# Expert weights as a dense matrix: two 128-column products per token accumulated in PSUM

## Chip, cores and metric

One NeuronCore of one Trainium2 chip runs the whole program. The metric is device time in microseconds (us) of one execution. For the kernel before, three runs are shown, with a median of 1796.3 us (1794.24 to 1799.25). A profiled execution of its own was recorded beside them.

## The reference, cut to what matters

A transformer block and a second block run over 256 tokens. The change lies in the last layer of the second block, `peer`, in which every token picks 8 x 16 = 128 of 16384 one-neuron experts through two tables of 128 keys, and sums their outputs:

```
experts = e1 * N_KEYS + e2                      # N_KEYS = 128
g = softmax(cs)                                 # 128 weights a token
act = gelu(einsum('td,tkd->tk', xt, u_tab[et])) * gt
out = einsum('tk,tkd->td', act, v_tab[et])
```

## The kernel before, in words

The kernel doesn't gather. It computes the activation of **all** 16384 experts for all 256 tokens, multiplies it by a dense matrix of weights that is zero where an expert wasn't picked, and multiplies the result by all of `v_tab`. Everything is 32-bit; a matrix product is made of three (`mm3`, lines 303 to 306): each operand is split into a rounded high half and the low rest, both of type fp32r, and high x high, high x low and low x high are added up in PSUM.

Three stages matter here.

- **Experts in.** `experts_in` (line 1389) takes two tiles of `u_tab` (128 experts each), makes two products of 8 x 3 = 24 matmuls of 256 columns with the tokens (`gemm_w`, lines 308 to 312; in the trace lines 304, 305 and 306), applies gelu on ScalarE (line 1396) and stores the pair to DRAM. Each tile of 128x1024 weights comes through `Stream`: a load on the SP queue, a rounding copy on ScalarE (line 250, tile `wh`) and a subtraction on VectorE (line 252, tile `wl`), four tiles ahead, each with four buffers. There are 64 such pairs; the first ones run beside the routing, the rest beside the dense weights.
- **Dense weights.** `weights_dense` (line 1508) is a generator that is stepped from inside the loop of line 1572: after each `gemm_w`, `paced` (line 1547) steps it about three times, so its instructions stand in every engine's queue between those of two expert tiles. It takes one token a step. For four tokens VectorE makes four one-hot matrices of the first index (line 1518, tile `oh1`, two buffers). For each token VectorE makes a 128x256 tile (line 1523, tile `ow`, six buffers): the one-hot of the second index times the high half of the weight, and beside it the same times the low half. Four steps later (`LAG`, line 29) TensorE multiplies the two (line 1533): one matmul of 256 columns, 128 of the high and 128 of the low half, with the first one-hot as the stationary operand. Two tokens fill a PSUM bank of 512 columns (tag `acc`, three banks). When a bank is full ScalarE copies the low parts to `gd` (line 1538), and VectorE adds the high parts to them (line 1539).
- **Experts out.** When all tokens are done, `act_split` (line 1560) multiplies the stored activations by `gd` on GpSimd (line 1564), splits them, and the products with `v_tab` follow.

The order on each engine is the order in which the program issues (`manual_schedule`): an instruction that waits holds up all that stands behind it on its engine.

Of the kernel before, what the change touches and what calls it, by code (L numbers as in the profile page):

```python
# [16 lines left out]
ALU = mybir.AluOpType  # L17
# [4 lines left out]
T = 256  # L22
# [7 lines left out]
ONE = 4  # L30
# [253 lines left out]
def body(ctx, tc, a, o, upto=99):  # L284
    nc = tc.nc
# [6 lines left out]
    def psum(tag):  # L292
        return PS.tile([128, 512], F32, tag=tag, name=tag, bufs={"mm": 2, "acc": 3, "od": 1, "tr": 2}[tag])

    def accs():
        return [psum("acc"), psum("acc"), psum("acc"), psum("od")]
# [37 lines left out]
    def gemm_rows(acc, w, xh, xl, start, stop):  # L334
        h, lo = w
        for tt in range(2):
            ts_ = slice(tt * 128, tt * 128 + 128)
            for hf in range(2):
                cs = slice(hf * 512, hf * 512 + 512)
                mm3(acc[2 * tt + hf], xh[:, ts_], xl[:, ts_], h[:, cs], lo[:, cs], start, stop)  # L340

    def split(h, lo, src, eng=None):
        nc.scalar.copy(h, src)  # L343
        (eng or nc.vector).tensor_tensor(lo, src, h.bitcast(F32), op=ALU.subtract)  # L344
# [32 lines left out]
    def gain(i, pool):  # L377
        g = pool.tile([128, D], F32, tag="gain", name="gain", bufs=1)
        nc.gpsimd.dma_start(g, a["gains"][i:i + 1, :].to_broadcast([128, D]))
        return g  # L380
# [283 lines left out]
    with tc.tile_pool(name="mix", bufs=1) as MP:  # L664
# [251 lines left out]
        for n, (s, g) in enumerate(MIX_ORDER):  # L916
# [6 lines left out]
            if n == 2:  # L923
                pump.add(subln())
                for gg in range(3):
                    pt = psum("mm")
# [19 lines left out]
        for c in range(8):  # L946
            pt = psum("mm")
# [11 lines left out]
        for b in range(4):  # L959
            if b % 2 == 0:  # L960
                w = ws.next()
            pt = psum("tr" if b % 2 else "mm")
# [11 lines left out]
        g = gain(POSTM, MP)  # L974
# [88 lines left out]
    with tc.tile_pool(name="b2", bufs=1) as BP:  # L1063
# [277 lines left out]
        for i in range(4):  # L1341
            pt = psum("mm")
# [4 lines left out]
            t = th[:, 2 * i:2 * i + 2, :]  # L1347
# [10 lines left out]
        for c in range(8):  # L1358
            pt = psum("mm")
# [29 lines left out]
    def experts_in(i, between=pump.step):  # L1389
        pt = psum("mm")  # L1390
        gemm_w(pt[:, :T], ws.next(), xs_x)
        between()
        gemm_w(pt[:, T:], ws.next(), xs_x)
        st = PP.tile([128, 2, T], F32, tag="st", name="st", bufs=2)
        last[i] = st
        nc.scalar.activation(st, pt.rearrange("p (e t) -> p e t", e=2), AF.Gelu_apprx_tanh)  # L1396
        if i < 62:
            nc.scalar.dma_start(stored[i // 4][:, 2 * (i % 4):2 * (i % 4) + 2, :], st)
# [3 lines left out]
    with tc.tile_pool(name="route", bufs=1) as RP:  # L1402
# [3 lines left out]
        v = RP.tile([128, 2, 16, 16], F32, name="v")  # L1406
# [22 lines left out]
        for b in range(16):  # L1429
            if b < 2:  # L1430
                pt = first[b]
            else:
                pt = psum("mm")
# [69 lines left out]
    with tc.tile_pool(name="dense", bufs=1) as GP:  # L1503
        gd = GP.tile([128, 128, T], F32, name="gd")

        wp = GP.tile([128, 2, 128], F32R, name="wp")

        def weights_dense():

            o1s, ohs = {}, {}  # L1510
            for t in range(T + LAG):
                if t < T:
                    tt, tl = divmod(t, 128)
                    if tl == 0:
                        split(wp[:, 0], wp[:, 1], eT[tt][:, 2])
                    if t % ONE == 0:
                        o1 = GP.tile([128, ONE, 128], F32R, tag="oh1", name="oh1", bufs=2)
                        nc.vector.tensor_tensor(o1, iota[:, None, :].to_broadcast([128, ONE, 128]),  # L1518
                                                eT[tt][:, 0, tl:tl + ONE, None].to_broadcast([128, ONE, 128]),
                                                op=ALU.is_equal)  # L1520
                        o1s[t // ONE] = o1
                    oh = GP.tile([128, 2, 128], F32R, tag="ow", name="oh2", bufs=6)
                    nc.vector.scalar_tensor_tensor(oh, iota[:, None, :].to_broadcast([128, 2, 128]),  # L1523
                                                   eT[tt][:, 1, tl:tl + 1],
                                                   wp[:, :, tl:tl + 1].bitcast(F32).to_broadcast([128, 2, 128]),
                                                   op0=ALU.is_equal, op1=ALU.mult)
                    ohs[t] = oh
                u = t - LAG
                if u >= 0:
                    if u % 2 == 0:  # L1530
                        pt = psum("acc")
                    oh = ohs.pop(u)
                    nc.tensor.matmul(pt[:, u % 2 * T:u % 2 * T + T], o1s[u // ONE][:, u % ONE],  # L1533
                                     oh.rearrange("p n e -> p (n e)"), start=True, stop=True)
                    if u % 2 == 1:
                        v = pt.rearrange("p (t n e) -> p n e t", t=2, n=2)
                        g = gd[:, :, u - 1:u + 1]
                        nc.scalar.copy(g, v[:, 1])  # L1538
                        nc.vector.tensor_tensor(g, v[:, 0], g, op=ALU.add)  # L1539
                yield  # L1540

        pump.add(weights_dense())
        left = 128 - 2 * n_in[0]
        total = T + LAG
        busy = left - 4

        def paced(i):
            for _ in range(min(i + 1, busy) * total // busy - min(i, busy) * total // busy):
                pump.step()

        sv = {}

        def fetch(b):
            if b < 16:
                sv[b] = P0.tile([128, 8, T], F32, tag="lT" if b % 2 else "hT", name="sv")
                nc.gpsimd.dma_start(sv[b][:, :8 if b < 15 else 4, :], stored[b])

        order = list(range(124, 128)) + list(range(124))

        def act_split(n):  # L1560
            e = order[n]
            src = last[e // 2] if e >= 124 else sv[e // 8][:, e % 8 - e % 2:e % 8 - e % 2 + 2, :]
            if e % 2 == 0:
                nc.gpsimd.tensor_tensor(src, src, gd[:, e:e + 2, :], op=ALU.mult)  # L1564
            ah = GP.tile([128, T], F32R, tag="ow", name="ah", bufs=6)
            al = GP.tile([128, T], F32R, tag="ow", name="al", bufs=6)
            split(ah, al, src[:, e % 2])
            if e % 8 == 7 and e < 120:
                fetch(e // 8 + 2)
            return ah, al  # L1570

        for i in range(left // 2):
            experts_in(n_in[0] + i, lambda: paced(2 * i))
            paced(2 * i + 1)
            if i == left // 2 - 2:
                pump.drain()
                ws.pool_every = 0
                nxt = [act_split(0), act_split(1)]
        fetch(0)
        fetch(1)  # L1580
        acc = accs()
        for n in range(126):
            nxt.append(act_split(n + 2))
            ah, al = nxt.pop(0)
            gemm_rows(acc, ws.next(), ah, al, n == 0, False)
        gf = P0.tile([128, D], F32, tag="raw", name="gf", bufs=RAW)
        nc.scalar.dma_start(gf, a["gains"][FINAL:FINAL + 1, :].to_broadcast([128, D]))
        x2 = [P0.tile([128, D], F32, tag="raw", name="x2", bufs=RAW) for tt in range(2)]
        for tt in range(2):
            nc.scalar.dma_start(x2[tt], res[tt * 128:(tt + 1) * 128, :])  # L1590
        finish(acc, [(ws.next(), *nxt[n]) for n in range(2)])
        jk = P0.tile([128, 1024], F32, tag="wh", name="jk", bufs=NH)
        ys = [P0.tile([128, D], F32, tag="wl", name="ys", bufs=NL) for tt in range(2)]
        rs = [None, None]

        def scaled(tt, hf):
            y = ys[tt][:, HALVES[hf]]
            if hf:
                nc.scalar.activation(y, y, AF.Copy, scale=rs[tt])
            else:  # L1600
                nc.vector.tensor_scalar(y, y, rs[tt], None, op0=ALU.mult)
            (nc.scalar if tt and hf else nc.sync).dma_start(o[tt * 128:tt * 128 + 128, HALVES[hf]], y)

        for tt in range(2):
            fn = RowNorm(GP, lambda hf: x2[tt][:, HALVES[hf]], jk[:, :512])
            for hf, sl in enumerate(HALVES):
                nc.vector.tensor_tensor(x2[tt][:, sl], acc[2 * tt + hf], x2[tt][:, sl], op=ALU.add)
                fn.half(hf)
            if tt:
                scaled(0, 0)  # L1610
                scaled(0, 1)
            for sl in HALVES:
                nc.vector.tensor_tensor(ys[tt][:, sl], x2[tt][:, sl], gf[:, sl], op=ALU.mult)
            rs[tt] = fn.root()
        for hf in range(2):
            scaled(1, hf)
# [19 lines left out]
```

## Time and profile before

| what | us |
|---|---|
| median of 3 runs | 1796.3 |
| profiled execution, its own time | 1792.96 |
| span of the profiled execution, first to last instruction | 1791.1 |
| PE busy (97% of the span) | 1729.7 |
| DVE busy (74%) | 1332.6 |
| ACT busy (52%) | 936.1 |
| POOL busy (18%) | 319.1 |

PE is TensorE's matmuls, PEld its weight loads, DVE VectorE, ACT ScalarE, POOL GpSimd. The dense weights are made from 1146 to 1424 us of the span. The granted clock of TensorE is 0.991 over the span, 1.0 being 2.4 GHz. A duration of an instruction reaches from its start to its end; neighbours on one engine overlap, so the time that an instruction takes up in a full queue is the distance from its start to the next one's, which is shorter. A timeline merges neighbours of one line: "0.97 ... x8" is the time from the first start to the last end of eight.

### The profile page before, as it was taken

Reading aid. Unit: us, or ns where it says so; the run is one execution under the profiler, and the core shown is the slowest. Engines: PE = TensorE matmul, PEld = TensorE weight load, DVE = VectorE, ACT = ScalarE, POOL = GpSimd, SP = SyncE. Lnnn points to the kernel's source line nnn. Section 1 sums busy time; section 2 is a strip of 40 time slices with the busy share of each in tenths; the row PEclk is TensorE's granted clock in tenths of the full one; section 3 lists DMA queues with packets and bytes.
Section 4 is the critical chain, followed back from the end, with each engine's and each line's share of the span. In section 5 each row is a group of like instructions: output and inputs, shape, how many; then the busy total and the mean of one; then the engine's idle time right before and its main releaser. Section 6 shows DMA issues by size and latency. Waiting matters only on the chain.

```text
span 1791.1 us, 30504 instructions
## 1 busy us (share of the span) xinstructions
PE 1729.7 (97%) x11790; PEld 1581.5 (88%) x11794; DVE 1332.6 (74%) x2177; ACT 936.1 (52%) x1515; POOL 319.1 (18%) x249
## 2 busy tenths in 40 slices
PE   8999999999999999999899889899999999999998
PEld 7999888999899987997799889899999988888886
DVE  5665668855665645888767999899999977776766
ACT  5544556545464435685545345455555545545554
POOL 3000133221300101000003344100000033333332
PEclk9999999999999999999999999999999999999999
DMA  7656453444476653553255456566665677777775
GB/s 235 191 174 196 148 164 106 138 134 156 162 216 190 198 166 117 167 188 106 91 180 191 140 189 219 199 195 190 200 198 191 199 249 252 243 241 240 244 239 173
DMA packets 93410, 332.08 MB, mean 185 GB/s; under 512 B 10552, under 2 KB 10707, under 8 KB 90960
## 3 DMA queue, kind: packets, MB, share of 16 engines
q1 hardware_dynamic: 79488, 287.73, 50.0%
q0 software_dynamic: 3696, 21.67, 3.6%
q10 hardware_dynamic: 10080, 20.71, 3.2%
q8 instruction: 93, 1.52, 0.4%
q14 instruction: 53, 0.43, 0.1%
HBM read 311.73 MB, written 18.35 MB: 184 GB/s over the span
## 4 chain that ended last, share of the span: by engine, by line
PE 62%; DVE 26%; issue 4%; ACT 4%; DMA 3%; POOL 1%; ACTq 0%; POOLq 0%; SPq 0%; DVEq 0%
PE mm L304 10%; PE mm L306 9%; PE mm L305 9%; PE acc L306 7%; PE acc L305 7%; PE acc L304 7%; DVE wl L252 7%; DVE oh L1523 5%; DVE gd L1539 2%; PE od L304 2%; PE od L305 2%; PE od L306 2%; DVE oh L1518 2%; ACT wh L250 2%; DMA raw<-in_us_dram 1%
## 5 line engine op out<-in xcount | busy, mean ns | idle before, releaser
L252 DVE TENSOR_TENSOR wl<-raw,wh 128x1024 fp32r<-128x1024 f32 x502 | 651.9, 1302 | 281.7 <-ACT wh L250 279.6
L306 PE MATMUL mm<-hT,wl 128*128 128x256 f32 (+1 forms) x2496 | 706.5, 283 | 10.7 <-DVE wl L252 10.7
L304 PE MATMUL mm<-hT,wh 128*128 128x256 f32 (+1 forms) x2496 | 715.0, 286 | 1.7 <-ACT rxp L1227 1.3
L250 ACT CAST wh<-raw 128x1024 fp32r<-128x1024 f32 x544 | 570.4, 1052 | 262.1 <-DMA raw<-in_us_dram 73.2
L305 PE MATMUL mm<-lT,wh 128*128 128x256 f32 (+1 forms) x2496 | 706.3, 283 | 0.0
L306 PEld LDWEIGHTS mm<-hT,wl 128*128 128x128 f32 x2496 | 475.5, 191 | 11.7 <-DVE wl L252 11.7
L304 PEld LDWEIGHTS mm<-hT,wh 128*128 128x128 f32 x2496 | 475.1, 190 | 10.4 <-issue 5.5
L305 PEld LDWEIGHTS mm<-lT,wh 128*128 128x128 f32 x2496 | 473.9, 190 | 3.4 <-issue 1.4
L306 PE MATMUL acc<-wh,al 128*128 128x512 f32 x516 | 202.1, 392 | 0.5 <-DVE al L344 0.5
L304 PE MATMUL acc<-wh,ah 128*128 128x512 f32 x516 | 202.0, 391 | 0.0
L305 PE MATMUL acc<-wl,ah 128*128 128x512 f32 x516 | 201.5, 391 | 0.1
L252 POOL TENSOR_TENSOR wl<-raw,wh 128x1024 fp32r<-128x1024 f32 x42 | 111.1, 2646 | 198.0 <-ACT wh L250 198.0
L1523 DVE SCALAR_TENSOR_TENSOR oh<-iota,eT,wp 128x256 fp32r<-128x256 f32 x256 | 117.3, 491 | 0.0
L306 PEld LDWEIGHTS acc<-wh,al 128*128 128x128 f32 x516 | 96.8, 188 | 21.8 <-DVE al L344 1.1
L305 PEld LDWEIGHTS acc<-wl,ah 128*128 128x128 f32 x516 | 96.9, 188 | 20.2 <-DVE wl L252 0.5
L304 PEld LDWEIGHTS acc<-wh,ah 128*128 128x128 f32 x516 | 96.9, 188 | 19.2 <-issue 0.3
L343 ACT CAST ah<-sv 128x256 fp32r<-128x256 f32 x124 | 50.5, 407 | 120.6 <-PE od L305 44.8
L344 DVE TENSOR_TENSOR al<-sv,ah 128x256 fp32r<-128x256 f32 x124 | 77.5, 625 | 39.0 <-ACT ah L343 38.8
L1564 POOL TENSOR_TENSOR sv<-sv,gd 128x512 f32<-128x512 f32 x62 | 101.3, 1660 | 5.7 <-DMA sv<-act 5.3
L1396 ACT ACTIVATE st<-mm 128x512 f32<-128x512 f32 x64 | 38.3, 598 | 75.9 <-PE mm L306 75.8
L1538 ACT COPY gd<-acc 128x256 f32<-128x256 f32 x128 | 46.5, 402 | 59.3 <-PE acc L1533 42.9
L417 POOL TENSOR_SCALAR ssq<-ssq 128x1 f32<-128x1 f32 x18 | 8.1, 450 | 356.4 <-ACT junk L415 327.6
(388 smaller groups left out, 2198.5 us busy)
## 6 DMA issues: line engine op xcount, KB each, us to landing
raw<-in_ws_dram SPq DMA_DIRECT2D x288, 512.0 KB, 3.8
raw<-in_us_dram SPq DMA_DIRECT2D x128, 512.0 KB, 3.6
raw<-in_vs_dram SPq DMA_DIRECT2D x128, 512.0 KB, 4.3
act<-st ACTq DMA_DIRECT2D x62, 256.0 KB, 2.7
sv<-act POOLq DMA_DIRECT2D x15, 1024.0 KB, 7.7
gate_w<-in_gate_w_dram ACTq DMA_DIRECT2D x2, 1024.0 KB, 5.6
gain<-in_gains_dram POOLq DMA_DIRECT2D x3, 512.0 KB, 6.7
res<-x SPq DMA_DIRECT2D x2, 512.0 KB, 4.2
```

Source lines behind the costliest of these rows:

```text
L250: nc.scalar.copy(h, raw)
L252: eng.tensor_tensor(lo, raw, h.bitcast(F32), op=ALU.subtract)
L304: nc.tensor.matmul(out, lh, rh, start=start, stop=False)
L305: nc.tensor.matmul(out, lh, rl, start=False, stop=False)
L306: nc.tensor.matmul(out, ll, rh, start=False, stop=stop)
L343: nc.scalar.copy(h, src)
L344: (eng or nc.vector).tensor_tensor(lo, src, h.bitcast(F32), op=ALU.subtract)
L1396: nc.scalar.activation(st, pt.rearrange("p (e t) -> p e t", e=2), AF.Gelu_apprx_tanh)
L1518: nc.vector.tensor_tensor(o1, iota[:, None, :].to_broadcast([128, ONE, 128]), eT[tt][:, 0, tl:tl + ONE, None].to_broadcast([128, ONE, 128] ...
L1523: nc.vector.scalar_tensor_tensor(oh, iota[:, None, :].to_broadcast([128, 2, 128]), eT[tt][:, 1, tl:tl + 1], wp[:, :, tl:tl + 1].bitcast(F3 ...
L1538: nc.scalar.copy(g, v[:, 1])
L1564: nc.gpsimd.tensor_tensor(src, src, gd[:, e:e + 2, :], op=ALU.mult)
```

## The change

The tile of line 1523 is unchanged. In place of one matmul of 256 columns a token gets two of 128, the one of the high and the one of the low half, both with the same stationary operand and into the same 128 columns of PSUM, where they add up. A bank now holds four tokens. When it is full, one ScalarE copy of 512 columns writes the four tokens to `gd`; the copy and the addition of every second token are gone.

```diff
                 u = t - LAG
                 if u >= 0:
-                    if u % 2 == 0:
+                    q = u % 4
+                    if q == 0:
                         pt = psum("acc")
                     oh = ohs.pop(u)
-                    nc.tensor.matmul(pt[:, u % 2 * T:u % 2 * T + T], o1s[u // ONE][:, u % ONE],
-                                     oh.rearrange("p n e -> p (n e)"), start=True, stop=True)
-                    if u % 2 == 1:
-                        v = pt.rearrange("p (t n e) -> p n e t", t=2, n=2)
-                        g = gd[:, :, u - 1:u + 1]
-                        nc.scalar.copy(g, v[:, 1])
-                        nc.vector.tensor_tensor(g, v[:, 0], g, op=ALU.add)
+                    for n in range(2):
+                        nc.tensor.matmul(pt[:, q * 128:q * 128 + 128], o1s[u // ONE][:, u % ONE], oh[:, n],
+                                         start=q == 0 and n == 0, stop=q == 3 and n == 1)
+                    if q == 3:
+                        nc.scalar.copy(gd[:, :, u - 3:u + 1], pt.rearrange("p (t e) -> p e t", t=4))
                 yield
```

## Rows read from the trace of the kernel before

**Rows 1.** Windows: stretch, then busy us (count) of each engine, clock, DMA share, GB/s.

```profile
1146.00:1424.00 278.00, 272.16 (x2244) 267.02 (x2243) 277.99 (x532) 148.34 (x254) 0.00 (x0) 1.00 0.61 198
```

**Rows 2.** Chain of waits of the stretch 1146 to 1424 us, by line.

```profile
by line: DVE oh L1523 34.4%; DVE wl L252 20.3%; DVE gd L1539 15.5%; DVE oh L1518 13.8%; issue 12.9%; PE mm L304 0.9%; PE mm L305 0.9%; PE mm L306 0.9%; PE acc L1533 0.5%; DVE wp L344 0.1%
```

**Rows 3.** Timeline of DVE: start, duration, line, tile; one of each kind.

```profile
1313.60 0.45 DVE L1539 TENSOR_TENSOR gd<-acc,gd 128x256 f32<-128x256 f32 x1
1313.94 0.70 DVE L1518 TENSOR_TENSOR oh<-iota,eT 128x512 fp32r<-128x512 f32 x1
1314.54 0.49 DVE L1523 SCALAR_TENSOR_TENSOR oh<-iota,eT,wp 128x256 fp32r<-128x256 f32 x1
1314.94 1.23 DVE L252 TENSOR_TENSOR wl<-raw,wh 128x1024 fp32r<-128x1024 f32 x1
1316.07 0.49 DVE L1523 SCALAR_TENSOR_TENSOR oh<-iota,eT,wp 128x256 fp32r<-128x256 f32 x1
```

**Rows 4.** Groups, 1146 to 1424 us: count, busy us, mean ns, idle before, releasers.

```profile
L304 PE MATMUL mm<-hT,wh 128*128 128x256 f32 x663 | 185.8, 280 | 0.0
...
L1523 DVE SCALAR_TENSOR_TENSOR oh<-iota,eT,wp 128x256 fp32r<-128x256 f32 x256 | 117.3, 491 | 0.0
L252 DVE TENSOR_TENSOR wl<-raw,wh 128x1024 fp32r<-128x1024 f32 x83 | 102.0, 1229 | 0.0
...
L1539 DVE TENSOR_TENSOR gd<-acc,gd 128x256 f32<-128x256 f32 x128 | 57.4, 449 | 0.0
L1533 PE MATMUL acc<-oh,oh 128*128 128x256 f32 x256 | 50.8, 291 | 5.8 <-DVE oh L1523 4.2 <-ACT gd L1538 0.5 <-ACT st L1396 0.4
L1538 ACT COPY gd<-acc 128x256 f32<-128x256 f32 x128 | 46.5, 402 | 59.3 <-PE acc L1533 42.9 <-ACT st L1396 16.5
L1518 DVE TENSOR_TENSOR oh<-iota,eT 128x512 fp32r<-128x512 f32 x64 | 44.4, 694 | 0.0
L1533 PEld LDWEIGHTS acc<-oh,oh 128*128 128x128 f32 x256 | 38.4, 188 | 11.0 <-issue 7.0 <-ACT st L1396 1.2 <-ACT gd L1538 1.2
L1396 ACT ACTIVATE st<-mm 128x512 f32<-128x512 f32 x42 | 25.2, 600 | 69.6 <-PE mm L306 69.6
```

**Rows 5.** Timeline of PE, first and last of 20 matmuls without a gap.

```profile
1311.81 0.28 PE L305 MATMUL mm<-lT,wh 128*128 128x256 f32 x1
...
1314.06 0.28 PE L306 MATMUL mm<-hT,wl 128*128 128x256 f32 x1
```

**Rows 6.** Waits, 1146 to 1424 us: who for whom, total us, times, longest.

```profile
PEld acc L1533 <- issue: 7.0, 20, 0.5
PE acc L1533 <- DVE oh L1523: 4.2, 17, 0.6
...
PEld acc L1533 <- ACT gd L1538: 1.2, 2, 0.6
```

**Rows 7.** Page, costliest groups: matmuls and weight loads of the expert products.

```profile
L304 PE MATMUL mm<-hT,wh 128*128 128x256 f32 (+1 forms) x2496 | 715.0, 286 | 1.7 <-ACT rxp L1227 1.3
...
L304 PEld LDWEIGHTS mm<-hT,wh 128*128 128x128 f32 x2496 | 475.1, 190 | 10.4 <-issue 5.5
L305 PEld LDWEIGHTS mm<-lT,wh 128*128 128x128 f32 x2496 | 473.9, 190 | 3.4 <-issue 1.4
```

**Rows 8.** Timeline of weight loads ahead of narrow matmuls, elsewhere in the span.

```profile
358.52 0.97 PEld L882 LDWEIGHTS od<-vz,eT 128*128 128x128 f32 x8
567.10 0.57 PEld L509 LDWEIGHTS tr<-ident,meta 16*128 16x128 f32 x8 [0.37 <-issue]
1008.52 0.53 PEld L1421 LDWEIGHTS acc<-keys,qb 128*128 128x128 f32 x4
```

**Rows 9.** One line's instructions: count, duration min/median/max ns, first and last start.

```profile
L882 PEld LDWEIGHTS od<-vz,eT x64: 190/192/192, 358.5 to 440.7; 128*128 128x128 f32 x64
L882 PE MATMUL od<-vz,eT x64: 222/275/275, 358.6 to 440.7; 128*128 128x64 f32 x64
L509 PEld LDWEIGHTS tr<-ident,meta x8: 133/137/138, 567.1 to 567.5; 16*128 16x128 f32 x8
```

## The prediction

> **What bounds the kernel now.** I read the stretch in which the dense weights are made, 1146 to 1424 us; the change touches nothing outside it. In the windows view DVE is busy for 277.99 of its 278 us and PE for 272.16, while ACT has 148.34 and POOL nothing [rows 1]: two engines are full, and the first question is which one has room to give.
>
> The chain of waits names DVE: of these 278 us, lines 1523, 252, 1539 and 1518 hold 84%, PE under 4% [rows 2]. The DVE timeline gives what each instruction takes up in the full queue, start to next start: line 1539 0.34 us (1313.60 to 1313.94), line 1518 0.60, line 1523 0.40, line 252 1.13 [rows 3]. With the counts of the stretch (128, 64, 256, 83) [rows 4] that is 43.5 + 38.4 + 102.4 + 93.8 = 278.1 us. So DVE has no room at all, and the addition that the change removes is 43.5 us of it.
>
> But PE stands right behind. From 1311.81 to 1314.06 us, 20 matmuls of 256 columns follow each other without a gap, 19 distances in 2.25 us: 0.118 us each [rows 5]. The stretch has 2244 matmuls [rows 1], 256 of them of line 1533 [rows 4], so 1988 of the experts. 2244 x 0.118 = 264.8 us: PE's own floor lies only 13.2 us under the 278. If DVE cost nothing, 13.2 us is all that could be won, 0.7% of the run. The waits view tells what these are: line 1533 waits for its tile from DVE, 4.2 us at the matmul, and 7.0 us at its weight load under "issue", which I count to the same cause since that load stands behind the matmul that waits; waits for ACT are the small rest, such as 1.2 us for line 1538 [rows 6].
>
> **The change, part by part.**
>
> *Removed, DVE:* 128 additions, 43.5 us of queue. DVE needs 234.6 us in the stretch afterwards and no longer waits for ACT's copy.
>
> *Moved, ACT:* 128 copies of 256 columns at 402 ns (51.5 us by mean) become 64 copies of 512 columns. The nearest row with that shape, also from PSUM, is line 1396 at 600 ns [rows 4]: 38.4 us. ACT is idle for nearly half of the stretch [rows 1], so I cost this at nothing. If that cover were gone, each copy would hold the weight cast of line 250 behind it for 0.2 us more, 64 x 0.2 = 12.8 us at most.
>
> *Added waits:* a copy now waits for the eighth product of a bank, behind it the cast of line 250 and the gelu of line 1396. Tiles are cast four ahead, about 13 us, so a later copy delays no expert product. PE takes a new bank every four tokens out of three, so the copy has eight tokens' time to free one. On DVE the tile of line 1523 still needs one of six buffers, that of the token six steps back, whose second product now ends one product later: 0.1 us, behind a queue with 43 us of new room. I cost all of these at nothing. No DMA is added or moved.
>
> *Changed, PE:* this decides. 256 products of 256 columns become 512 of 128, each with a weight load of its own: lines 304 and 305 use the same stationary half in succession, and each has as many weight loads (2496) as line 304 has matmuls (2496) [rows 7], so a repeated stationary operand is loaded again. What does an fp32r product of 128 columns take? The trace has none. The nearest rows:
>
> - Line 882 multiplies with 64 columns of plain f32. A call of plain f32 shows as two records (32 of its calls write the tile `od`, and they have 64 [rows 9]). Eight of its loads of 128x128 take 0.97 us from first start to last end, the last lasting 0.19: (0.97 - 0.19) / 7 = 0.111 us from load to load [rows 8]. Half as many columns as line 1421's don't make it shorter: there four loads give (0.53 - 0.19) / 3 = 0.113 [rows 8]. So it is the load that sets the pace below 128 columns, not the columns.
> - The loads of line 1533 last 188 ns [rows 4], as line 882's 192 [rows 9]: the same kind of load.
> - Low end: line 509's transposes of 16x16, (0.57 - 0.14) / 7 = 0.061 us [rows 8], but their loads last 137 ns [rows 9], another kind.
> - High end: line 1421's plain f32 product of 128 columns needs two records, 2 x 0.113 = 0.226 us.
>
> I take 0.112 us, by line 882, whose load is the like one; within this reading 0.108 to 0.118, the last being today's distance. Then PE pays 512 x 0.112 = 57.3 us in place of 256 x 0.118 = 30.2: **27.1 us more** on the engine that becomes the only bound. Halving the columns saves nothing, since the second load takes the time that they give back.
>
> The Trainium skill ("TensorE: Matmul & The Clock Gate", section "Back-to-back issue gap") gives about 81 ns a matmul for a stream of load and 128-column matmul pairs; by it the 512 products would take an estimated 41.5 us in place of 57.3. No run here shows such an fp32r product, and the rows of lines 882 and 1421 lie a third above that figure.
>
> *Sum.* Expert products 1988 x 0.118 = 234.6 us, dense products 57.3, and of the 13.2 us of gaps some 3 that name ACT stay while those for DVE go: 294.9 in place of 278, **+16.9 us**. The profiled execution took 1792.96 us (span 1791.1 and 1.9 around it), so 1809.9 in its terms. The median of the runs shown is 3.3 us above it: 1796.3 + 16.9 = **1813 us**.
>
> **The rivals.**
>
> 1. *Faster: DVE was the bound, and a narrow product costs its columns.* For it: the chain of waits. If loads hide as line 509's do, the products take 512 x 0.061 = 31.2 us, the gaps go, and the stretch takes 234.6 + 31.2 + 3 = 268.8: -9.2 us, 1787 us. Against it: line 882's loads. It decides from a product under about 0.07 us.
> 2. *No change: the second load of a pair is cheap* because the same stationary is there. 256 x (0.112 + 0.061) = 44.3, the stretch 281.9: +3.9 us, 1800 us. Against it: in rows 5 lines 304 and 305 keep one distance throughout though their stationary is the same. The skill's figure above falls on this side, at an estimated 279 us for the stretch.
> 3. *Much slower: the halved product runs as plain f32 does* (four passes in place of one). 512 x 0.226 = 115.7, the stretch 353: +75 us, 1872 us. For it: all other matmuls of 128 columns in this kernel are plain f32, so none shows that fp32r keeps its rate there.
> 4. *It doesn't relieve DVE as it says:* PE's slower burst holds the buffers of line 1523, and the gaps stay. The stretch is then 234.6 + 60.4 + 13.2 = 308.2 at 0.118 a product: +30.2, 1826 us. That is the upper end of my own case.
>
> **How the numbers follow.** My case (with rival 4 as its end) has 0.80, rival 1 0.08, rival 2 0.06, rival 3 0.06. About 0.3% (5.4 us) is what a measurement can tell from no change. Slower: 0.86; same: 0.06; faster: 0.08. The range is that of my case alone, which leaves 0.2 out: its lower end 234.6 + 512 x 0.108 with no gaps left = 289.9, +11.9, its upper end +30.2, and about 3 us on either side for the spread of the runs shown: 1805 to 1830.
>
> **What would show it.** Right: PE full in the stretch, which lasts about 295 us; 512 loads of line 1533 some 0.11 us apart; DVE with over 40 us idle, waiting for PE's buffers; the chain in the stretch by PE, not DVE; 64 copies near 0.6 us that nobody waits for; all later stages as long as now, only later. Wrong: loads of line 1533 well under 0.1 us apart (rivals 1 and 2) or twice as many records of it (rival 3); gaps before line 1533 that still name DVE (rival 4); a later stage that moves by itself.

## The result, and the profile after

The change made the kernel **slower by 0.8%**: a median of 1808.38 us (1806.39 to 1812.43, six runs) against 1793.92 us before (six runs, the three shown above among them), ratio 1.0082 with a 95% interval of 1.0071 to 1.0094. That is 14.5 us. The profiled execution of the kernel after took 1812.43 us, with a span of 1810.7.

The windows view of the stretch of the dense weights and, below it, the chain of waits in that stretch. Columns of the first row: stretch, its length, then busy us and count of PE, PEld, DVE, ACT and POOL, clock, DMA share, GB/s.

```profile
1150.00:1442.00 292.00, 292.00 (x2496) 291.91 (x2495) 240.96 (x404) 142.41 (x189) 0.00 (x0) 1.00 0.59 189
...
by line: PE mm L304 28.1%; PE mm L306 26.9%; PE mm L305 26.9%; PE acc L1535 18.1%
```

The two engines have changed places. Before, DVE was full and PE had 6 us without a matmul [rows 1]; now PE has none, and DVE is idle for 51 us. The chain, which DVE's lines held [rows 2], is PE's alone.

The new line of the products in the view of one line's instructions (count, duration min/median/max, first and last start), and the groups of the stretch that answer to [rows 4]:

```profile
L1535 PEld LDWEIGHTS acc<-oh,oh x512: 186/192/192, 1150.8 to 1441.0; 128*128 128x128 f32 x171
...
L1523 DVE SCALAR_TENSOR_TENSOR oh<-iota,eT,wp 128x256 fp32r<-128x256 f32 x256 | 111.7, 477 | 0.0
L252 DVE TENSOR_TENSOR wl<-raw,wh 128x1024 fp32r<-128x1024 f32 x83 | 101.5, 1223 | 45.6 <-ACT wh L250 44.9
L250 ACT CAST wh<-raw 128x1024 fp32r<-128x1024 f32 x82 | 86.2, 1051 | 12.3 <-PE mm L305 7.8 <-DVE oh L1523 4.1 <-DMA raw<-in_us_dram 0.5
L1535 PE MATMUL acc<-oh,oh 128*128 128x128 f32 x512 | 66.5, 266 | 0.0
...
L1538 ACT COPY gd<-acc 128x512 f32<-128x512 f32 x64 | 37.6, 587 | 62.0 <-PE acc L1535 50.4 <-ACT st L1396 11.5
L1396 ACT ACTIVATE st<-mm 128x512 f32<-128x512 f32 x42 | 25.2, 600 | 75.8 <-PE mm L306 75.8
```

The same view of the old line of the products, in the kernel before:

```profile
L1533 PEld LDWEIGHTS acc<-oh,oh x256: 186/188/192, 1146.5 to 1422.0; 128*128 128x128 f32 x128
```

From the first to the last load of the dense products it is 1150.8 to 1441.0, 290.2 us; before it was 1146.5 to 1422.0, 275.5 us. **The stretch grew by 14.7 us, which is the whole loss.** (The profiled executions differ by more, 19.6 us of span: 4.3 us lie ahead of the stretch and hold nothing that was changed.) The matmuls of line 1535 wait for nobody, where line 1533 had waited for DVE [rows 4, 6]. DVE now waits in front of line 252, 44.9 us, for the cast of line 250. That cast is held up mostly by its place on ScalarE, behind gelus (line 1396) and copies (line 1538) that wait 75.8 and 50.4 us for PE; its own wait for a buffer from PE is 7.8 us. DVE, which was full, now idles behind PE.

What a product takes is read from the timeline of the weight loads (start, duration, line), one burst of six (three tokens) with its neighbours and the start of the next burst:

```profile
1302.46 0.19 PEld L306 LDWEIGHTS mm<-hT,wl 128*128 128x128 f32 x1
1302.58 0.76 PEld L1535 LDWEIGHTS acc<-oh,oh 128*128 128x128 f32 x6
1303.25 0.19 PEld L304 LDWEIGHTS mm<-hT,wh 128*128 128x128 f32 x1
...
1306.09 0.31 PEld L1535 LDWEIGHTS acc<-oh,oh 128*128 128x128 f32 x2
```

Six loads take 1303.25 - 1302.58 = 0.67 us, **0.112 us each**. From burst to burst it is 3.51 us: 24 expert matmuls at 0.118 and six products at 0.113.

### The profile page after: what moved, and what is told of

It reads as the page before. It is cut to its first block, busy times and chain, and to the rows that moved or that the text cites. A ratio compares the mean times of both kernels' runs of the same rounds, so it can differ in the third digit from the quotient of the medians.

```text
span 1810.7 us, 30888 instructions
## 1 busy us (share of the span) xinstructions
PE 1748.9 (97%) x12046; PEld 1605.2 (89%) x12050; DVE 1295.3 (72%) x2049; ACT 929.6 (51%) x1451; POOL 315.4 (17%) x249
## 4 chain that ended last, share of the span: by engine, by line
PE 80%; DVE 12%; ACT 3%; issue 2%; DMA 2%; POOL 1%; POOLq 0%; ACTq 0%; DVEq 0%
PE mm L304 15%; PE mm L306 14%; PE mm L305 14%; PE acc L306 7%; PE acc L305 7%; PE acc L304 7%; DVE wl L252 3%; PE acc L1535 3%; PE od L304 2%; PE od L305 2%; PE od L306 2%; ACT wh L250 1%; PE tr L1288 1%; DVE nb L720 1%; DMA raw<-in_ws_dram 1%
## 5 line engine op out<-in xcount | busy, mean ns | idle before, releaser
L343 ACT CAST ah<-sv 128x256 fp32r<-128x256 f32 x124 | 50.4, 406 | 125.1 <-PE od L305 50.5
L1523 DVE SCALAR_TENSOR_TENSOR oh<-iota,eT,wp 128x256 fp32r<-128x256 f32 x256 | 111.7, 477 | 0.0
L1538 ACT COPY gd<-acc 128x512 f32<-128x512 f32 x64 | 37.6, 587 | 62.0 <-PE acc L1535 50.4
```

Source lines behind the costliest of these rows:

```text
L1538: nc.scalar.copy(gd[:, :, u - 3:u + 1], pt.rearrange("p (t e) -> p e t", t=4))
```

## The experiments

All ratios are to the kernel before, with a 95% interval; "length" is from the first to the last load of the dense products, which includes 82 expert tiles, 82 x 24 = 1968 matmuls.

| kernel | median us | ratio | length us |
|---|---|---|---|
| before | 1793.9 | 1 | 275.5 |
| after | 1808.4 | 1.0082 (1.0071 to 1.0094) | 290.2 |
| e1, without the addition | 1783.0 | 0.9949 (0.9932 to 0.9965) | 263.7 |
| e2, two products, addition kept | 1809.2 | 1.0090 (1.0073 to 1.0107) | 290.2 |
| e3, 64 columns | 1811.8 | 1.0109 (1.0092 to 1.0126) | 289.1 |
| e4, 256 columns | 1814.5 | 1.0117 (1.0101 to 1.0134) | 294.2 |
| e5, bf16 halves | 1787.7 | 0.9959 (0.9945 to 0.9972) | 267.1 |
| e6, addition on GpSimd | 1831.6 | 1.0201 (1.0183 to 1.0220) | 310.5 |
| e7, plain f32 | 1809.9 | 1.0074 (1.0057 to 1.0091) | 290.2 |
| e8, every fourth subtraction on GpSimd | 1820.6 | 1.0131 (1.0114 to 1.0148) | 296.9 |

The change has two halves, the addition that goes and the products that double. The first two kernels make one half each.

### e1: the addition goes, the products stay

```diff
                         nc.scalar.copy(g, v[:, 1])
-                        nc.vector.tensor_tensor(g, v[:, 0], g, op=ALU.add)
```

> The kernel before without the addition on VectorE (line 1539), the products unchanged; the high halves are left out of the dense weights. My theory: VectorE was the bound of the stretch and TensorE stood 13 us behind it, so this alone gives 10 to 13 us (ratio 0.993 to 0.9945), the stretch falls to about 266 us, PE has no gaps. Rival (the addition was hidden, the stretch was TensorE's already): within 0.3%.

Windows, the products' line and one wait of this kernel:

```profile
1148.00:1412.00 264.00, 263.95 (x2225) 263.83 (x2226) 237.47 (x402) 146.07 (x251) 0.00 (x0) 1.00 0.70 208
...
L1533 PEld LDWEIGHTS acc<-oh,oh x256: 186/188/193, 1148.0 to 1411.7; 128*128 128x128 f32 x128
...
PE acc L1533 <- DVE oh L1523: 0.5, 1, 0.5
```

10.3 us faster than the runs of the kernel before that were made beside it (1793.35 us). The stretch is 11.8 us shorter, and PE now fills it: (1968 + 256) x 0.118 = 262.4 us of matmuls in 263.7. So DVE did set the pace before, and the 43.5 us of additions taken from it were worth only the 12 us by which PE stood behind it. As a whole time it is the small end of what I had expected: 10.3 us of 10 to 13, and a ratio of 0.9949 just outside 0.993 to 0.9945.

### e2: the products double, copies and addition stay

```diff
-                    nc.tensor.matmul(pt[:, u % 2 * T:u % 2 * T + T], o1s[u // ONE][:, u % ONE],
-                                     oh.rearrange("p n e -> p (n e)"), start=True, stop=True)
+                    for n in range(2):
+                        c0 = u % 2 * T + n * 128
+                        nc.tensor.matmul(pt[:, c0:c0 + 128], o1s[u // ONE][:, u % ONE], oh[:, n], start=True, stop=True)
```

> The kernel before with two products of 128 columns in place of one of 256, into the places that the one wrote; copies and additions stay. My theory: each product is paced by its weight load at 0.113 us, so TensorE needs 234 + 58 = 292 us beside a VectorE that needs 278: at least +14 us, up to +27 if the gaps stay (ratio 1.008 to 1.015). Rival (a repeated stationary operand or a narrow product is cheap, and the loss comes from the new bank layout and the single copy): within 0.3%.

```profile
1146.00:1436.00 290.00, 290.00 (x2480) 290.00 (x2479) 280.43 (x527) 149.05 (x251) 0.00 (x0) 1.00 0.60 188
...
L1535 PEld LDWEIGHTS acc<-oh,oh x512: 188/192/193, 1145.9 to 1436.1; 128*128 128x128 f32 x171
```

The same 290.2 us as the kernel after, though DVE still adds and is busy for 280 of 290 us. So the loss is the products' alone; the new layout of the banks and the single copy have no part in it. And with the products doubled, removing the addition is worth nothing: DVE's 280 us hide under PE's 290.

### e3 and e4: the same 512 products with 64 and with 256 columns

```diff
-                        nc.tensor.matmul(pt[:, q * 128:q * 128 + 128], o1s[u // ONE][:, u % ONE], oh[:, n],
-                                         start=q == 0 and n == 0, stop=q == 3 and n == 1)
+                        c0 = n * 64
+                        nc.tensor.matmul(pt[:, q * 128 + c0:q * 128 + c0 + 64], o1s[u // ONE][:, u % ONE],
+                                         oh[:, n, c0:c0 + 64], start=q == 0 and n == 0, stop=q == 3 and n == 1)
```

```diff
-                        nc.tensor.matmul(pt[:, q * 128:q * 128 + 128], o1s[u // ONE][:, u % ONE], oh[:, n],
+                        nc.tensor.matmul(pt[:, q % 2 * T:q % 2 * T + T], o1s[u // ONE][:, u % ONE],
+                                         oh.rearrange("p n e -> p (n e)"),
                                          start=q == 0 and n == 0, stop=q == 3 and n == 1)
```

> The kernel after with the same 512 products, each of 64 columns (the left 64 of the high half, the right 64 of the low half; the rest of the weights is left out). My theory: the load paces the product, so halving the columns changes nothing: same time as the kernel after, 0.108 to 0.113 us from load to load, ratio to the kernel before 1.007 to 1.009. Rival (the columns pace it): 512 x 0.027 us less, 14 us under the kernel after, ratio about 1.000.

> The kernel after with the same 512 products, each of 256 columns (high and low side by side, two tokens on each other, so the dense weights are meaningless). My theory: 0.118 us a product in place of 0.113: 2 to 3 us over the kernel after, ratio to the kernel before 1.009 to 1.011. Rival (the columns pace it): 512 x 0.053 us more, 27 us over the kernel after, ratio about 1.023.

The products' line with 64 columns, and a burst of six loads:

```profile
L1536 PEld LDWEIGHTS acc<-oh,oh x512: 186/192/193, 1148.2 to 1437.3; 128*128 128x128 f32 x171
L1536 PE MATMUL acc<-oh,oh x512: 191/277/297, 1148.3 to 1437.4; 128*128 128x64 f32 x171
...
1302.95 0.76 PEld L1536 LDWEIGHTS acc<-oh,oh 128*128 128x128 f32 x6
```

With 256 columns:

```profile
L1535 PEld LDWEIGHTS acc<-oh,oh x512: 187/189/193, 1148.4 to 1442.6; 128*128 128x128 f32 x171
...
1302.22 0.79 PEld L1535 LDWEIGHTS acc<-oh,oh 128*128 128x128 f32 x6
```

From 64 to 128 columns the length changes by 1.1 us (289.1 to 290.2), from 128 to 256 by 4.0: 512 products of four times as many columns cost 5.1 us more, 10 ns each. Within a burst it is (0.76 - 0.19) / 5 = 0.114 us from load to load with 64 columns as with 128, and (0.79 - 0.19) / 5 = 0.120 with 256. If columns set the pace, e3 would have been 14 us under the kernel after and e4 27 us over it. **The columns don't set it: a product has a fixed price, and each product brings one load.** That the price is the load's, and not another fixed cost of a pair of load and matmul, these two runs don't show.

Both whole times came out above what I had expected: a ratio of 1.0109 where 1.007 to 1.009 had been forecast, 3 us too much, and 1.0117 where it was 1.009 to 1.011, 1 us. e3 is 3 us over the kernel after by its median, though its stretch is 1 us shorter; the two were run at different times, and their intervals meet. Neither comes near its rival (1.000 and 1.023).

Where the columns catch up can be read from wider matmuls of the kernel before, 25 of 512 columns without a gap:

```profile
1599.73 0.39 PE L305 MATMUL acc<-wl,ah 128*128 128x512 f32 x1
...
1605.17 0.39 PE L305 MATMUL acc<-wl,ah 128*128 128x512 f32 x1
```

That is 5.44 / 24 = 0.227 us each. Half of it, an estimate for 256 columns by the columns alone, is 0.113 us, the price of a narrow product. So at 256 columns the two are about equal.

### e7: one plain f32 product in place of two fp32r ones

```diff
...
-                    nc.vector.scalar_tensor_tensor(oh, iota[:, None, :].to_broadcast([128, 2, 128]),
-                                                   eT[tt][:, 1, tl:tl + 1],
-                                                   wp[:, :, tl:tl + 1].bitcast(F32).to_broadcast([128, 2, 128]),
-                                                   op0=ALU.is_equal, op1=ALU.mult)
+                    nc.vector.tensor_scalar(oh, iota, eT[tt][:, 1, tl:tl + 1], eT[tt][:, 2, tl:tl + 1],
+                                            op0=ALU.is_equal, op1=ALU.mult)
...
-                    for n in range(2):
-                        nc.tensor.matmul(pt[:, q * 128:q * 128 + 128], o1s[u // ONE][:, u % ONE], oh[:, n],
-                                         start=q == 0 and n == 0, stop=q == 3 and n == 1)
+                    nc.tensor.matmul(pt[:, q * 128:q * 128 + 128], o1s[u // ONE][:, u % ONE], oh,
+                                     start=q == 0, stop=q == 3)
```

Beside the lines shown, the split of the weight goes and both one-hots become tiles of plain f32.

> The kernel after with one product of plain f32 and 128 columns a token in place of two fp32r products of its halves; no split of the weight, VectorE's tile is 128 columns wide. My theory: a plain f32 product is two loads and two records at 0.113 us, so TensorE needs what it needs in the kernel after, and VectorE's further relief changes nothing: ratio to the kernel before 1.007 to 1.010. Rival (fp32r is the cheaper form at 128 columns): slower than the kernel after by more than 5 us, ratio over 1.011.

```profile
L1529 PEld LDWEIGHTS acc<-oh,oh x512: 186/192/193, 1148.5 to 1438.7; 128*128 128x128 f32 x171
```

256 products, 512 loads, and again 290.2 us. One plain f32 product of 128 columns costs what two fp32r products do, and it shows two loads each. So rival 3 had the price of plain f32 right, and the one of fp32r wrong.

### e5: the halves in bf16

```diff
-        wp = GP.tile([128, 2, 128], F32R, name="wp")
+        wp = GP.tile([128, 2, 128], BF16, name="wp")
...
-                        split(wp[:, 0], wp[:, 1], eT[tt][:, 2])
+                        nc.scalar.copy(wp[:, 0], eT[tt][:, 2])
+                        nc.vector.tensor_tensor(wp[:, 1], eT[tt][:, 2], wp[:, 0], op=ALU.subtract)
...
-                        o1 = GP.tile([128, ONE, 128], F32R, tag="oh1", name="oh1", bufs=2)
+                        o1 = GP.tile([128, ONE, 128], BF16, tag="oh1", name="oh1", bufs=2)
...
-                    oh = GP.tile([128, 2, 128], F32R, tag="ow", name="oh2", bufs=6)
+                    oh = GP.tile([128, 2, 128], F32R, tag="ow", name="oh2", bufs=6).bitcast(BF16)[:, :, :128]
...
-                                                   wp[:, :, tl:tl + 1].bitcast(F32).to_broadcast([128, 2, 128]),
+                                                   wp[:, :, tl:tl + 1].to_broadcast([128, 2, 128]),
```

If the load is the price, a shorter load must give the time back. The one-hots hold only 0 and 1, which bf16 holds exactly; the weight keeps two bf16 pieces in place of two fp32r ones, and how exactly they hold it no number here tells.

> The kernel after with its one-hots and weight halves in bf16 (high = the weight rounded to bf16, low = the rest rounded to bf16); still 512 products of 128 columns into PSUM, one copy for four tokens, no addition. Both theories say that the load paces a product; what a bf16 load takes no row shows. If it is shorter than an fp32r one, down to the columns' own time, about half of today's 0.113 us: 0.056 us a product, the stretch near 264 us from first to last load, ratio to the kernel before 0.992 to 0.996, faster than both kernels. If a bf16 load takes 0.11 us as well: ratio 1.007 to 1.010 like the kernel after. By the Trainium skill (TensorE: Matmul & The Clock Gate, Back-to-back issue gap) an estimated 0.081 us: ratio 0.998 to 1.001.

Windows, the products' line, and two bursts on the timeline of the loads:

```profile
1149.00:1416.00 267.00, 266.50 (x2477) 262.91 (x2478) 238.04 (x403) 141.16 (x188) 0.00 (x0) 1.00 0.68 205
...
L1536 PEld LDWEIGHTS <-oh x512: 95/98/102, 1149.0 to 1416.1; 128*128 128x128 bf16 x171
...
1301.88 0.19 PEld L306 LDWEIGHTS mm<-hT,wl 128*128 128x128 f32 x1
1302.11 0.34 PEld L1536 LDWEIGHTS <-oh 128*128 128x128 bf16 x6
1302.40 0.19 PEld L304 LDWEIGHTS mm<-hT,wh 128*128 128x128 f32 x1
...
1305.35 0.34 PEld L1536 LDWEIGHTS <-oh 128*128 128x128 bf16 x6
```

**Faster than both kernels**, by 7.7 us than the runs of the one before beside it (1795.34 us). A load lasts 98 ns in place of 192. From burst to burst it is 3.24 us; less 24 x 0.118 that leaves 0.41 us for six products, 0.068 each, the change of type at either end included. The stretch is 8.4 us shorter than before and 23.1 shorter than the kernel after, with the same number of products, the same copy and the same layout. So adding up in PSUM can win; with operands of 32 bits the narrow products cost more than the addition.

The stretch was expected near 264 us and took 267.1: the change of type between the expert matmuls and the products had not been priced. And one thing stays open. e5 changes the type of the loads and of the matmuls together, so it fits the load as the price, but it doesn't part the load from another fixed cost of a 32-bit product. How long a load's record lasts doesn't settle it either. In the trace of the kernel before, four transposes of 32-bit tiles with 128 columns have loads of 0.14 us, shorter than the 0.19 of the products:

```profile
392.56 0.46 PEld L796 LDWEIGHTS tr<-ident,ov 128*128 128x128 f32 x4
```

They still come (0.46 - 0.14) / 3 = 0.107 us apart.

### e6 and e8: relieving VectorE by GpSimd instead

Both keep the single product of 256 columns. e6:

```diff
-                        nc.vector.tensor_tensor(g, v[:, 0], g, op=ALU.add)
+                        if u < T - 16:
+                            hi = gd[:, :, u + 7:u + 9]
+                            nc.scalar.copy(hi, v[:, 0])
+                            nc.gpsimd.tensor_tensor(g, hi, g, op=ALU.add)
+                        else:
+                            nc.vector.tensor_tensor(g, v[:, 0], g, op=ALU.add)
```

> The kernel before with the addition on GpSimd for all but the last tokens: ScalarE copies both halves out of PSUM, the high one into columns of gd that later tokens overwrite, and GpSimd adds them. My theory: VectorE loses its 43 us, TensorE keeps its 118 ns products, ScalarE takes 51 us more out of some 130 idle: ratio 0.994 to 0.997 as without the addition. Rival (VectorE slows beside a busy GpSimd: line 252 takes 2.01 us beside it in the trace of before, 1.23 alone, and 120 additions keep GpSimd busy for about 100 us): the gain is given back, ratio 0.998 to 1.005.

e8:

```diff
         pump.add(weights_dense())
+        ws.pool_every = 4
```

> The kernel before with every fourth subtraction of line 252 on GpSimd within the stretch, nothing else changed. My theory: VectorE was the bound, 20 subtractions at 1.13 us are 23 us of it, more than the 13 us by which TensorE lies behind: ratio 0.994 to 0.997, without a second load. Rival (VectorE slows beside GpSimd by as much as it is relieved): within 0.3%.

Windows, the products' loads and three groups of e6:

```profile
1146.00:1456.00 310.00, 282.56 (x2223) 268.37 (x2222) 309.64 (x404) 180.18 (x370) 146.92 (x120) 1.00 0.54 175
...
L1533 PEld LDWEIGHTS acc<-oh,oh x256: 185/188/193, 1145.8 to 1456.3; 128*128 128x128 f32 x128
...
L1523 DVE SCALAR_TENSOR_TENSOR oh<-iota,eT,wp 128x256 fp32r<-128x256 f32 x253 | 157.7, 662 | 0.0
L1542 POOL TENSOR_TENSOR gd<-gd 128x256 f32<-128x256 f32 x120 | 146.9, 1239 | 153.6 <-ACT gd L1541 153.5
...
L1518 DVE TENSOR_TENSOR oh<-iota,eT 128x512 fp32r<-128x512 f32 x63 | 62.4, 991 | 0.0
```

Windows and the products' loads of e8, then its timeline: one subtraction on POOL and what DVE did meanwhile, after one pair of line 1523 without it; and a second subtraction, with line 1539 beside it:

```profile
1149.00:1446.00 297.00, 272.98 (x2222) 268.20 (x2223) 294.22 (x507) 147.35 (x250) 52.02 (x20) 0.99 0.59 182
...
L1533 PEld LDWEIGHTS acc<-oh,oh x256: 186/188/330, 1149.1 to 1446.0; 128*128 128x128 f32 x128
...
1302.84 0.88 DVE L1523 SCALAR_TENSOR_TENSOR oh<-iota,eT,wp 128x256 fp32r<-128x256 f32 x2
...
1305.71 2.99 DVE L1523 SCALAR_TENSOR_TENSOR oh<-iota,eT,wp 128x256 fp32r<-128x256 f32 x2
...
1305.61 2.41 POOL L252 TENSOR_TENSOR wl<-raw,wh 128x1024 fp32r<-128x1024 f32 x1 [12.71 <-ACT wh L250]
...
1189.76 0.44 DVE L1539 TENSOR_TENSOR gd<-acc,gd 128x256 f32<-128x256 f32 x1
1190.11 2.65 DVE L1523 SCALAR_TENSOR_TENSOR oh<-iota,eT,wp 128x256 fp32r<-128x256 f32 x2
...
1189.49 2.59 POOL L252 TENSOR_TENSOR wl<-raw,wh 128x1024 fp32r<-128x1024 f32 x1 [11.96 <-ACT wh L250]
```

My theory failed in both: it counted what VectorE sheds and put what GpSimd takes from VectorE at nothing. The rival was right in kind and far too mild in size. GpSimd's 2.41 us put 2.1 us on a pair of line 1523 that otherwise takes 0.88: DVE stands still for nearly the whole GpSimd instruction.

- **e8.** If all twenty cost as much, an estimate, that is 42 us, against the 20 x 1.13 = 23 that they give back. The windows agree: DVE's busy time rose from 277.99 to 294.22 us with those 23 taken off it, so about 39 were put on. The stretch grew by 21.4. Some 3 us on PE are of another kind: twice, after PE had stood for 2.1 us, the granted clock fell to its level of 1.2 GHz (0.98 in the mean from 1250 to 1350 us, 0.96 from 1400 to 1446), and 30 expert loads followed each other at 0.21 us in place of 0.118.
- **e6.** Line 1523 goes from 491 to 662 ns, line 1518 from 694 to 991, and DVE is full again. These two alone put 44 + 19 = 63 us on DVE, against the 120 x 0.34 = 41 that the additions give back; the stretch grew by 35.0.

Not every instruction of DVE is held. Line 1539 reads one operand from PSUM (`acc`) and one from SBUF (`gd`); inside a GpSimd instruction of 2.59 us it takes its usual 0.44, and the pair of line 1523 behind it takes 2.65. The Trainium skill ("SBUF — State Buffer", section "Who interferes with whom") says that a VectorE instruction with two SBUF inputs contends with a GpSimd instruction that reads SBUF; line 1523 has two (`iota` and `wp`), and the trace agrees, by the 2.1 us above.

## Why the prediction was right

- **The bound.** That DVE has no room and PE stands 13.2 us behind, e1 shows: 11.8 us of stretch and 10.3 us of time once DVE is relieved, and then a single gap of 0.5 us before line 1533 that names DVE.
- **The product.** Taken as 0.112 us by line 882's loads, measured 0.112 to 0.113 by the loads and 58.0 us in all (290.2 - 1968 x 0.118) where the sum had 57.3. That step decided, and e3, e4 and e7 bear it out: with 64, 128 and 256 columns, and for each of the two records of plain f32, a product takes nearly the same time. The reason given for it, the load, fits all of them and e5, but isn't parted from another fixed cost of a 32-bit product. The lower end of 0.108 was named without a row; it is the shortest distance that the loads of line 1535 show.
- **The gaps.** The sum kept 3 us of waits for ACT; none stayed. That is the difference between the +16.9 us of the sum and what the stretch lost, 58.0 - 256 x 0.118 - 13 = 14.8, with 0.7 us of the product term the other way. The median of 1813 us stood on 1796.3; six runs put the kernel before at 1793.9, which is the other half of the 4.6 us by which it was too high. So the measured 1808.4 lies near the lower end of 1805 to 1830.
- **The covers.** 64 copies at 587 ns (forecast 600) that nobody waits for; DVE idle as forecast, though in front of line 252 for ACT's cast rather than at PE's buffers: at the latter it waits only 1.4 us, before line 1518, so rival 4's burst holds nothing up. Later stages didn't move: from the last load of the products to the end of the span it is 369.1 us before and 369.7 after.
- **The rivals.** Rival 1 needs products at about 0.06 us, rival 2 every second one; in the kernel after no load of line 1535 follows another by less than 0.108 us, and the second of a pair, with the stationary operand already there, comes no sooner (0.114 on average) than the first of the next pair (0.111). It takes these pairs to rule rival 2 out: the one distance of lines 304 and 305 in rows 5 couldn't, since their 256 columns take about 0.113 us by themselves. The 81 ns of the Trainium skill ("TensorE: Matmul & The Clock Gate", "Back-to-back issue gap") is not the price of fp32r, which is 0.113 us here; bf16's 0.068 lies below it. By the section "LDWEIGHTS (loading the stationary operand)" of the same page of the Trainium skill a load of P columns takes P / 1.2 ns, for 128 columns an estimated 107 ns; the fp32r loads agree, from load to load, with 0.108 to 0.113 us, though each one's record lasts 0.19. The Trainium skill's section "Weight-path perf modes — Fast Weight Load (FWL) and DoubleRow" on that page gives faster loads of 128 columns to types that aren't FP32, and e5's bf16 agrees, 98 ns a record in place of 192.

## What to carry to other kernels

Before a wide product is cut into narrow ones, price the product with its weight load, not its columns: here an fp32r product cost 0.114 us with 64 and with 128 columns and 0.120 with 256, so that up to about 256 columns halving it nearly doubled the bill. When one engine is full, read how far behind the next one stands: that distance (13 us here), not the work removed (43 us), is the most that relief can give. For a stream of products that must be narrow, measure a shorter type: here bf16 took the stretch from 290.2 to 267.1 us.

## What the runs showed that I had not expected

Bf16 products of 128 columns go at 0.068 us with the change of type included, against 0.113 for fp32r. Two of them take PE little more than one fp32r product of 256 columns (0.136 us against 0.118), and since they need no addition the stretch is 8.4 us shorter. And a GpSimd instruction held VectorE for nearly its whole length (2.1 of 2.41 us), which made it worse than no relief for a full VectorE whose instructions, most of them, read two tensors from SBUF: the stretch grew by 21.4 us in e8 and 35.0 in e6.
